# Issue orders of ACT, DVE and the queue in a fused attention and convolution step: five places moved

## The chip, the cores and the metric

The kernel runs on one core of a Trainium2 chip. The metric is the device time of one execution in microseconds (us); three runs were taken, and their median counts. The engines are PE (TensorE), DVE (VectorE), ACT (ScalarE), POOL (GpSimd) and SP (SyncE, which issues the transfers). In the rows of the profile PEld is the weight load of PE and SPq the issue on SP's queue.

## The reference, cut to what matters

```python
h = x / rms(x) * norm_g                              # x: 1024 prompt frames, 32 sample frames; D = 1024
q, k, v, f, ga, ua, ub, gb, ma, mb = split(h @ w_in) # each 1024 wide, f 16
q, k = rmsnorm(q) * q_g / 8, rmsnorm(k) * k_g        # per head, 16 heads of 64
o = softmax(q k^T + C[t] - C[s], causal) v           # C = cumsum(logsigmoid(f + b_f))
conv = depthwise(ua * sigmoid(ub), 31 taps, causal)  # conv state in front for the sample frames
ya = (o * silu(ga)) @ w_pa
yb = (silu(layernorm(conv)) * silu(gb)) @ w_pb
y = x + (sigmoid(ma) * ya + sigmoid(mb) * yb) @ w_out
# outputs: y, k, v, logsigmoid(f), last 30 conv rows; the sample frames attend over 512 cached ones too
```

All of it is f32.

## The kernel before

Every f32 product is made of three fp32r matmuls. A value is split into a high part (a cast to fp32r on ACT) and a low part (value minus high part, on POOL for weights, on DVE or POOL for activations), and PE adds high x high, low x high and high x low (`mms`, L102, in the profile `pj<-xh,wh`, `pj<-xh,wl`, `pj<-xl,wh`). A block is 128 output channels: 8 contraction slices (kt) times 3 column thirds of 352 frames times 3 matmuls, 72 in all, with its own weights of 128 x 1024: one load of `raw` (L85), one cast to `wh` (L91), three subtractions to `wl` (L94).

In the order of time the stages are:

- `x_split` (L413 to L510): transposes of x (`ptx`, L436), its split into `xh` and `xl` (L438, L439) and the first convolution input. The roots of the rows' mean squares come from `newton` (L375 to L379), called for rows 256 to 639 as `steps_of[2]` behind slice 5; the `scale` calls (L407, L409) multiply rows of x by them, and the transposes of the next chunk read those.
- the blocks of u, v, k and q, with the 30 convolution taps of each channel block on DVE (L265) beside them. Finished taps are summed for the LayerNorm (`into_sums`, L236 to L248): a sum on DVE, a square on ACT (L242), a sum of squares.
- the eight ga blocks, then the opening of the attention: `most(h, j)` (L917 to L932) makes the scores of 128 queries against their keys (`psS`, L924, one PSUM bank for j under 4, two from 4 on), adds the causal mask on the last 128 keys (L927) and takes the negative maximum `nm` (L932); `least` (L934) transposes the maxima and writes them into the query tile `QA` (L937).
- sixteen heads, each in four steps of PE work: weights (`psT`, L946, L947, masked on DVE in L950; exponential on ACT into `pt`, L953; running sums `acc` on POOL, L956, L959), products with V (`po`, L970), the scores of the next head's maxima, and between them matmuls of the gate blocks gb, ma, mb (`fill`). Of the 24 gate blocks (numbered 0 to 23) 22 go between the heads. With every second head `sums` (L978 to L1000) makes the row sums of two heads on PE (`pl`, L982), their logarithm (L984) and reciprocal (L994) on ACT, the product `rs` with silu(ga) on POOL (L997) and the product with the heads' output `ot` on DVE (L998), one half at each of its steps, and the store `s_o` (L1000).
- gate blocks 22 and 23, and meanwhile `a_half` (L1165): the attention output comes back from `s_o` and is split into `ah` (ACT, L1169) and `al` (DVE, L1170), one slice for each 128 channels.
- `outproj` (L1202) for pa, pb and out, 8 blocks each (pa0 to pa7 and so on). Block 0 goes slice by slice over all three thirds, since its input is only just being made; the others third by third. Beside pa, `ln_out` (L1174) makes the LayerNorm output `c_h`, `c_l` from the kept convolution: DVE (L1178, L1179, L1182), SiLU on ACT (L1180, L1181), cast on ACT (L1186), subtraction on POOL (L1187). `mk_pa` loads the gate ma in three thirds and takes tanh on ACT (L1222); DVE multiplies PE's result by it (L1225).

The order on PE is the order of the code. On ACT, DVE, POOL and SP a scheduler sets it for the first stage, the attention and what follows, by priorities (`high_priority` puts the weights' load, cast and subtractions forward) and by `issue_after`, which puts an instruction behind another one of its engine. Raw weights rotate over a list of pools, `rawp`: `load_raw` takes the first and puts it at the end (L83 to L85). The list has the pools of the projections until `rawp.extend` (L1156) adds two, ahead of the last two gate blocks.

Of the kernel before, what the change touches and what calls it, by code (L numbers as in the profile page):

```python
# [48 lines left out]
def build(tc, xT, xt, wv, wf, ckT, cv, clT, stT, vec, cst, yT, kT, vO, lfO, cpT, csT):  # L49
# [38 lines left out]
    def split_w(raw, offset=2000):  # L88
        with tc.high_priority(offset=offset):
            wh = wp.tile([128, KT, 128], F32R, name="wh", tag="wh")  # L90
            nc.scalar.copy(wh, raw)  # L91
            wl = wp.tile([128, KT, 128], F32R, name="wl", tag="wl")
            for k0, k1 in WSP:
                nc.gpsimd.tensor_sub(wl[:, k0:k1, :], raw[:, k0:k1, :], f32(wh[:, k0:k1, :]))  # L94
        return wh, wl
# [11 lines left out]

    late = []
    chores = []
    pace = {"tick": 0, "n": 0, "rate": 0.0, "credit": 0.0}  # L110

    def later(n, fn):
# [88 lines left out]
            taps.pop(0)()  # L201

    PCS = ((0, T, 0), (T + 30, TS, T))
    sides = {}

    def shift_of(y):

# [28 lines left out]
    def into_sums(f, y):  # L236
        for o, n, a in PCS:
            if f == 0:
                nc.vector.tensor_copy(mean[:, a:a + n], y[:, o:o + n])
            else:  # L240
                nc.vector.tensor_add(mean[:, a:a + n], mean[:, a:a + n], y[:, o:o + n])
        nc.scalar.activation(y, y, AF.Square)  # L242
        eng = nc.vector if f == 6 else nc.gpsimd
        for o, n, a in PCS:
            if f == 0:
                eng.tensor_copy(rstd[:, a:a + n], y[:, o:o + n])
            else:
                eng.tensor_add(rstd[:, a:a + n], rstd[:, a:a + n], y[:, o:o + n])  # L248
        if f == 7:
            sides["ready"] = True  # L250
# [105 lines left out]
    def vcol(base, f):  # L356
        return vec_t[:, base + f:base + f + 1]
# [17 lines left out]
    def newton(out, v, y):  # L375

        nc.vector.tensor_mul(out, y, y)
        nc.vector.scalar_tensor_tensor(out, out, -0.5, v, op0=ALU.mult, op1=ALU.mult)
        nc.vector.scalar_tensor_tensor(out, out, 1.5, y, op0=ALU.add, op1=ALU.mult)  # L379

    half = slice(0, D // 2), slice(D // 2, D)
    rows = lambda t: min(128, TT - 128 * t)
# [27 lines left out]

    behind = []

    def x_split(c, ws, u, jobs):  # L413


        o, n = XCH[c]
# [16 lines left out]
        for kt in range(KT):  # L433
            pt = tr.tile([128, 512], F32, name="ptx", tag="tr") if kt % 3 == 2 else st.tile([128, 512], F32, name="ptx", tag="st")
            for j in range((n + 127) // 128):
                nc.tensor.transpose(pt[:, 128 * j:128 * j + 128],  # L436
                                    xtok[o // 128 + j][:, 128 * kt:128 * kt + 128], ident)
            nc.scalar.mul(xh[:, kt, sl], pt[:, :n], vcol(V_NG, kt))  # L438
            nc.vector.scalar_tensor_tensor(xl[:, kt, sl], pt[:, :n], vcol(V_NG, kt), f32(xh[:, kt, sl]),  # L439
                                           op0=ALU.mult, op1=ALU.subtract)  # L440
            for job in jobs.get(kt, ()):
                job()
            behind.append(lambda kt=kt: project(kt))
            if len(behind) > 2:
                behind.pop(0)()
# [41 lines left out]
    for f in range(8):  # L487
# [9 lines left out]
        3: [lambda: squares(3, sl=half[0]), lambda: squares(3, False, half[1], part),  # L497
            lambda: V.tensor_add(rs9[:, 3:4], rs9[:, 3:4], part)],
        4: [lambda: rooted(2, 3)],
        5: [lambda: steps_of[2](), lambda: scale(2, 0), lambda: scale(3, 0, True), lambda: scale(4, 0)],  # L500
        6: [lambda: scale(3, 1, True), lambda: scale(2, 1)],
        7: [lambda: scale(4, 1)]})
    x_split(1, ws0, u0, {
        0: [lambda: squares(5), lambda: squares(6, False)],
        1: [lambda: squares(7)],
# [405 lines left out]
    class Attend:  # L911
# [66 lines left out]
        def sums(self, other):  # L978
# [11 lines left out]
            for i, (c, e, acc) in enumerate(four):  # L990
                for u in range(2):
                    q = 64 * e + 32 * u
                    with tc.issue_after(sides["weights"].ins):
                        nc.scalar.activation(rs[c][q:q + 32, :], ln[32 * i:32 * i + 32, :], AF.Exp, scale=-1.0)  # L994
                if e:
                    osl = slice(c * 512, c * 512 + 512)
                    nc.gpsimd.tensor_mul(rs[c], rs[c], self.g[:, osl])  # L997
                    nc.vector.tensor_mul(ot[:, osl], ot[:, osl], rs[c])  # L998
                yield
            nc.sync.dma_start(s_o[self.head.h // 2, :, :T], ot)  # L1000

    PT = [ap.tile([128, 4 * n, 512], F32, name=f"pt{n}", bufs=1) for n in (1, 2)]
# [50 lines left out]
                att[h].most(j)  # L1053

    for j in range(4):
        most(0, j, 4 + j)
        fill(8 if j == 3 else 4)
    att[0].least(0)
    att[0].least(1)
# [2 lines left out]
    for h in range(H):  # L1062
# [4 lines left out]
        for s in range(4):  # L1067
# [35 lines left out]
            elif s == 2:  # L1103
                most(h + 1, 3)
                most(h + 1, 5)
                fill(2)
                if k - 2 in sample:
                    sample[k - 2].turn()
# [44 lines left out]
    pjC = Banks3()  # L1153
    sg2 = pool("sg2", 4, stack=p3, side="right")
    bg = pool("bg", 5, stack=p3, side="right")
    rawp.extend(pool(f"rw{i}", 1, stack=p3, side="right") for i in range(2))  # L1156

    def big(name):
        return bg.tile([128, TT], F32, name=name, tag="big")
# [34 lines left out]
        a_half(f)  # L1194
    while fills:
        last_gate()

    def ln_step(f):
        for g in LNO[f - 1]:
# [2 lines left out]
    def outproj(g, rh, rl, mk, between=lambda f: None):  # L1202

        w = split_w(load_raw((g, 0)))
        pss = [pjC.tile([128, CH], F32, name="pj", tag="pj") for _ in range(3)]
        for kt in range(KT):
            for c in range(3):
# [2 lines left out]
        with tc.high_priority(offset=4000):  # L1210
            for c in range(3):
                ev(c, csl(c), pss[c])
        for f in range(1, 8):
            between(f)
            proj((g, f), rh, rl, pjC, mk(f))


    def mk_pa(f):
        sma = [sg2.tile([128, CH], F32, name="sma", tag="sma") for _ in range(3)]
        for c in range(3):  # L1220
            nc.sync.dma_start(sma[c], s_g["ma"][f, :, csl(c)])
            nc.scalar.activation(sma[c], sma[c], AF.Tanh, scale=0.5)  # L1222

        def ev(c, sl, ps):
            nc.vector.scalar_tensor_tensor(sma[c], sma[c], 1.0, ps, op0=ALU.add, op1=ALU.mult)  # L1225
# [119 lines left out]
```

## Time and profile before

| what | us |
|---|---|
| three runs | 1391.07, 1395.28, 1392.76 |
| median | 1392.76 |
| the profiled execution | 1393.11 |
| its span, first to last instruction | 1391.0 |
| PE busy | 1367.7 (98%) |
| DVE, POOL, ACT busy | 895.2, 704.6, 567.3 |

The mean granted clock of PE was 0.996. A row of the timeline is start, duration, engine, line, operation, output and inputs, shapes, count, and in brackets the idle time ahead of it with the instruction that ended it. A row of the waits is the waiting engine and line, the one waited for, the total in us, the count, and the longest.

### The profile page before, as it was taken

What the parts mean: (1) busy time and instruction counts of PE and PEld (TensorE: products, weight loads), DVE (VectorE), ACT (ScalarE), POOL (GpSimd) and SP (SyncE); (2) the same over time, 40 slices, a digit from 0 to 9 for tenths busy, and PEclk for the clock granted to TensorE, in tenths of its full rate; (3) what the DMA queues carried; (4) which work ended last, traced back from release to release, by engine and by line L of the source; (5) the groups of instructions that cost most, each with busy time, mean ns of one, the idle gap of its engine ahead of it and who ended that gap; (6) DMA issues with size and microseconds to landing.
All of it is one profiled execution on the core that took longest, in us unless ns stands there. A gap on an engine that the chain in (4) does not pass through costs nothing.

```text
span 1391.0 us, 22743 instructions
## 1 busy us (share of the span) xinstructions
PE 1367.7 (98%) x8707; PEld 1277.9 (92%) x8707; DVE 895.2 (64%) x1173; ACT 567.3 (41%) x1061; POOL 704.6 (51%) x589
## 2 busy tenths in 40 slices
PE   8999999999999999999999999999999999999999
PEld 8999999999999999998777887878887899999998
DVE  6787787888898998757766675854553496133111
ACT  6422334646464642223434445443543665222100
POOL 3334254567585875336645664554554466255320
PEclk9999999999999999999999999999999999999999
DMA  4342343534342475234546655565642877444431
GB/s 184 98 143 88 123 113 103 161 89 138 103 158 90 129 196 161 88 111 105 151 119 173 143 137 137 135 172 138 159 116 77 298 252 259 139 151 141 143 107 48
DMA packets 102797, 193.85 MB, mean 139 GB/s; under 512 B 17504, under 2 KB 70624, under 8 KB 102688
## 3 DMA queue, kind: packets, MB, share of 16 engines
q1 hardware_dynamic: 102544, 192.32, 46.5%
q8 instruction: 69, 1.13, 0.3%
q14 instruction: 40, 0.33, 0.1%
q10 hardware_dynamic: 144, 0.07, 0.0%
HBM read 126.17 MB, written 66.17 MB: 138 GB/s over the span
## 4 chain that ended last, share of the span: by engine, by line
PE 88%; DVE 5%; ACT 2%; issue 2%; DMA 1%; POOL 1%; SPq 0%; DVEq 0%; ACTq 0%; POOLq 0%
PE pj L102 66%; PE pjv L591 7%; PE po L970 5%; PE psS L924 2%; PE psT L947 2%; PE psT L946 2%; DVE nm L932 1%; PE pl L982 1%; PE pst L708 1%; DVE y L265 1%; PE pst L707 1%; PE ptx L436 0%; ACT acc L994 0%; POOL wl L94 0%; PE po L908 0%
## 5 line engine op out<-in xcount | busy, mean ns | idle before, releaser
L102 PE MATMUL pj<-xh,wh 128*128 128x352 f32 (+2 forms) x1536 | 505.8, 329 | 4.5 <-ACT wh L91 3.7
L102 PE MATMUL pj<-xl,wh 128*128 128x352 f32 (+2 forms) x1536 | 496.5, 323 | 0.5 <-DVE xl L439 0.3
L102 PE MATMUL pj<-xh,wl 128*128 128x352 f32 (+2 forms) x1536 | 495.4, 323 | 1.5 <-POOL wl L94 1.5
L94 POOL TENSOR_TENSOR wl<-raw,wh 128x384 fp32r<-128x384 f32 (+1 forms) x258 | 323.8, 1282 | 331.9 <-ACT wh L91 303.0
L265 DVE SCALAR_TENSOR_TENSOR y<-u,vec_t,y 128x1086 f32<-128x1086 f32 x240 | 385.1, 1605 | 23.9 <-ACT y L262 19.6
L102 PEld LDWEIGHTS pj<-xh,wh 128*128 128x128 f32 x1536 | 289.6, 189 | 14.0 <-ACT wh L91 4.3
L102 PEld LDWEIGHTS pj<-xh,wl 128*128 128x128 f32 x1536 | 290.6, 189 | 3.0 <-POOL wl L94 2.2
L102 PEld LDWEIGHTS pj<-xl,wh 128*128 128x128 f32 x1536 | 290.1, 189 | 1.7 <-DVE xl L439 1.6
L959 POOL TENSOR_TENSOR acc<-acc,pt 128x512 f32<-128x512 f32 (+3 forms) x128 | 125.4, 980 | 38.7 <-ACT pt L953 32.7
L91 ACT CAST wh<-raw 128x1024 fp32r<-128x1024 f32 x86 | 90.0, 1046 | 108.9 <-PE pj L102 78.3
L953 ACT ACTIVATE pt<-psT 128x512 f32<-128x512 f32 x192 | 83.5, 492 | 43.1 <-DVE psT L950 18.0
L725 POOL TENSOR_TENSOR ql<-qn,qh 128x352 fp32r<-128x352 f32 (+1 forms) x48 | 65.9, 1372 | 65.9 <-ACT qh L724 53.1
L932 DVE TENSOR_REDUCE nm<-psS 128x1 f32<-128x128 f32 (+7 forms) x128 | 93.5, 751 | 1.8
L956 POOL TENSOR_TENSOR acc<-pt 128x512 f32<-128x512 f32 x32 | 44.7, 1398 | 80.2 <-ACT pt L953 80.2
L763 ACT COPY t<-pj 128x352 f32<-128x352 f32 x72 | 32.6, 452 | 129.1 <-PE pj L102 65.8
L927 DVE TENSOR_TENSOR psS<-psS,cmask 128x128 f32<-128x128 f32 x128 | 37.3, 296 | 61.5 <-PE psS L924 59.1
L970 PE MATMUL po<-pt,V 128*64 128x512 f32 (+1 forms) x384 | 73.2, 530 | 0.0
L591 PE MATMUL pjv<-vwh,xh 128*128 128x260 f32 x256 | 72.5, 283 | 0.0
L591 PE MATMUL pjv<-vwl,xh 128*128 128x260 f32 x256 | 72.4, 283 | 0.0
L591 PE MATMUL pjv<-vwh,xl 128*128 128x260 f32 x256 | 72.3, 282 | 0.0
L970 PEld LDWEIGHTS po<-pt,V 128*64 128x64 f32 x384 | 26.4, 138 | 43.3 <-issue 40.0
L1255 DVE SCALAR_TENSOR_TENSOR xres<-pj,xres 128x352 f32<-128x352 f32 x24 | 12.5, 525 | 80.4 <-PE pj L102 76.9
(215 smaller groups left out, 2399.7 us busy)
## 6 DMA issues: line engine op xcount, KB each, us to landing
raw<-wf SPq DMA_DIRECT2D x88, 512.0 KB
QB<-s_q SPq DMA_DIRECT2D x32, 256.0 KB
KB<-s_k SPq DMA_DIRECT2D x32, 256.0 KB
kT<-qn SPq DMA_DIRECT2D x8, 528.0 KB
s_ga<-t SPq DMA_DIRECT2D x24, 176.0 KB
s_gb<-t SPq DMA_DIRECT2D x24, 176.0 KB
s_ma<-t SPq DMA_DIRECT2D x24, 176.0 KB
s_mb<-t SPq DMA_DIRECT2D x24, 176.0 KB
```

Source lines behind the costliest of these rows:

```text
L91: nc.scalar.copy(wh, raw)
L94: nc.gpsimd.tensor_sub(wl[:, k0:k1, :], raw[:, k0:k1, :], f32(wh[:, k0:k1, :]))
L102: nc.tensor.matmul(ps, a[:, kt, :], b(kt, sl), start=(first and n == 0), stop=(last and n == N - 1))
L265: t = nc.vector.scalar_tensor_tensor(y, u[:, i:i + CW], w, y, op0=ALU.mult, op1=ALU.add)
L591: nc.tensor.matmul(ps[:, :VC], a, b, start=(n == 0), stop=(n == 23))
L725: nc.gpsimd.tensor_sub(ql[:, :n], qn[:, o], f32(qh[:, :n]))
L927: nc.vector.tensor_add(diag, diag, cmask)
L932: nc.vector.tensor_reduce(nm[:, r:r + 1], ps[:, :nb, :w], axis=AX.XY, op=ALU.max, negate=True)
L953: sides['weights'] = nc.scalar.activation(p[:, j, q0:], ps[:, q0:], AF.Exp)
L956: nc.gpsimd.tensor_add(self.acc[c], p[:, 0, :], p[:, 1, :])
L959: nc.gpsimd.tensor_add(a[:, q0:], a[:, q0:], p[:, j, q0:])
L970: nc.tensor.matmul(po[64 * o:64 * o + 64, q0:], V[:, j + o, hd], p[:, j + o, q0:], start=(j == 0), stop=(j == njb - 2), skip_group_check=True)
```

## The change

The edits are:

- `into_sums`: the square on ACT is put behind the cast of weights issued last before it (`sides["wh"]`).
- `x_split`: the three root operations of rows 256 to 639 go ahead of the `xl` of slice 5 instead of behind it.
- the opening: `most(0, 4 + j, j)` in place of `most(0, j, 4 + j)`.
- `sums`: the two products with `ot` come in two further steps behind the four reciprocals, and the attention loop takes one more step in its part s == 2.
- the two added raw pools join the rotation behind the last gate block, at its front.
- `outproj("pa")`: the weights of pa1 are loaded and split right behind pa0's, and those of block f + 1 ahead of the LayerNorm steps in front of block f (`split[g, f]` is where `proj` finds weights already split); and each tanh of ma is put behind the cast issued last.

```diff
--- before.py
+++ after.py
@@ -88,7 +88,7 @@
     def split_w(raw, offset=2000):
         with tc.high_priority(offset=offset):
             wh = wp.tile([128, KT, 128], F32R, name="wh", tag="wh")
-            nc.scalar.copy(wh, raw)
+            sides["wh"] = nc.scalar.copy(wh, raw)
             wl = wp.tile([128, KT, 128], F32R, name="wl", tag="wl")
             for k0, k1 in WSP:
                 nc.gpsimd.tensor_sub(wl[:, k0:k1, :], raw[:, k0:k1, :], f32(wh[:, k0:k1, :]))
@@ -107,6 +107,7 @@
 
     late = []
     chores = []
+    sides = {}
     pace = {"tick": 0, "n": 0, "rate": 0.0, "credit": 0.0}
 
     def later(n, fn):
@@ -201,7 +202,6 @@
             taps.pop(0)()
 
     PCS = ((0, T, 0), (T + 30, TS, T))
-    sides = {}
 
     def shift_of(y):
 
@@ -239,7 +239,8 @@
                 nc.vector.tensor_copy(mean[:, a:a + n], y[:, o:o + n])
             else:
                 nc.vector.tensor_add(mean[:, a:a + n], mean[:, a:a + n], y[:, o:o + n])
-        nc.scalar.activation(y, y, AF.Square)
+        with tc.issue_after(sides["wh"].ins):
+            nc.scalar.activation(y, y, AF.Square)
         eng = nc.vector if f == 6 else nc.gpsimd
         for o, n, a in PCS:
             if f == 0:
@@ -376,7 +377,7 @@
 
         nc.vector.tensor_mul(out, y, y)
         nc.vector.scalar_tensor_tensor(out, out, -0.5, v, op0=ALU.mult, op1=ALU.mult)
-        nc.vector.scalar_tensor_tensor(out, out, 1.5, y, op0=ALU.add, op1=ALU.mult)
+        return nc.vector.scalar_tensor_tensor(out, out, 1.5, y, op0=ALU.add, op1=ALU.mult)
 
     half = slice(0, D // 2), slice(D // 2, D)
     rows = lambda t: min(128, TT - 128 * t)
@@ -410,7 +411,7 @@
 
     behind = []
 
-    def x_split(c, ws, u, jobs):
+    def x_split(c, ws, u, jobs, ahead={}):
 
 
         o, n = XCH[c]
@@ -436,8 +437,11 @@
                 nc.tensor.transpose(pt[:, 128 * j:128 * j + 128],
                                     xtok[o // 128 + j][:, 128 * kt:128 * kt + 128], ident)
             nc.scalar.mul(xh[:, kt, sl], pt[:, :n], vcol(V_NG, kt))
-            nc.vector.scalar_tensor_tensor(xl[:, kt, sl], pt[:, :n], vcol(V_NG, kt), f32(xh[:, kt, sl]),
-                                           op0=ALU.mult, op1=ALU.subtract)
+            with ExitStack() as first:
+                if kt in ahead:
+                    first.enter_context(tc.issue_after(ahead[kt]().ins))
+                nc.vector.scalar_tensor_tensor(xl[:, kt, sl], pt[:, :n], vcol(V_NG, kt), f32(xh[:, kt, sl]),
+                                               op0=ALU.mult, op1=ALU.subtract)
             for job in jobs.get(kt, ()):
                 job()
             behind.append(lambda kt=kt: project(kt))
@@ -497,9 +501,9 @@
         3: [lambda: squares(3, sl=half[0]), lambda: squares(3, False, half[1], part),
             lambda: V.tensor_add(rs9[:, 3:4], rs9[:, 3:4], part)],
         4: [lambda: rooted(2, 3)],
-        5: [lambda: steps_of[2](), lambda: scale(2, 0), lambda: scale(3, 0, True), lambda: scale(4, 0)],
+        5: [lambda: scale(2, 0), lambda: scale(3, 0, True), lambda: scale(4, 0)],
         6: [lambda: scale(3, 1, True), lambda: scale(2, 1)],
-        7: [lambda: scale(4, 1)]})
+        7: [lambda: scale(4, 1)]}, {5: lambda: steps_of[2]()})
     x_split(1, ws0, u0, {
         0: [lambda: squares(5), lambda: squares(6, False)],
         1: [lambda: squares(7)],
@@ -993,10 +997,13 @@
                     with tc.issue_after(sides["weights"].ins):
                         nc.scalar.activation(rs[c][q:q + 32, :], ln[32 * i:32 * i + 32, :], AF.Exp, scale=-1.0)
                 if e:
-                    osl = slice(c * 512, c * 512 + 512)
-                    nc.gpsimd.tensor_mul(rs[c], rs[c], self.g[:, osl])
-                    nc.vector.tensor_mul(ot[:, osl], ot[:, osl], rs[c])
+                    nc.gpsimd.tensor_mul(rs[c], rs[c], self.g[:, c * 512:c * 512 + 512])
                 yield
+            for c in range(2):
+                osl = slice(c * 512, c * 512 + 512)
+                nc.vector.tensor_mul(ot[:, osl], ot[:, osl], rs[c])
+                if c == 0:
+                    yield
             nc.sync.dma_start(s_o[self.head.h // 2, :, :T], ot)
 
     PT = [ap.tile([128, 4 * n, 512], F32, name=f"pt{n}", bufs=1) for n in (1, 2)]
@@ -1053,7 +1060,7 @@
                 att[h].most(j)
 
     for j in range(4):
-        most(0, j, 4 + j)
+        most(0, 4 + j, j)
         fill(8 if j == 3 else 4)
     att[0].least(0)
     att[0].least(1)
@@ -1103,6 +1110,7 @@
             elif s == 2:
                 most(h + 1, 3)
                 most(h + 1, 5)
+                next(norm, None)
                 fill(2)
                 if k - 2 in sample:
                     sample[k - 2].turn()
@@ -1153,7 +1161,7 @@
     pjC = Banks3()
     sg2 = pool("sg2", 4, stack=p3, side="right")
     bg = pool("bg", 5, stack=p3, side="right")
-    rawp.extend(pool(f"rw{i}", 1, stack=p3, side="right") for i in range(2))
+    more = [pool(f"rw{i}", 1, stack=p3, side="right") for i in range(2)]
 
     def big(name):
         return bg.tile([128, TT], F32, name=name, tag="big")
@@ -1194,6 +1202,7 @@
         a_half(f)
     while fills:
         last_gate()
+    rawp[:0] = more
 
     def ln_step(f):
         for g in LNO[f - 1]:
@@ -1202,6 +1211,8 @@
     def outproj(g, rh, rl, mk, between=lambda f: None):
 
         w = split_w(load_raw((g, 0)))
+        if g == "pa":
+            split[g, 1] = split_w(load_raw((g, 1)))
         pss = [pjC.tile([128, CH], F32, name="pj", tag="pj") for _ in range(3)]
         for kt in range(KT):
             for c in range(3):
@@ -1211,6 +1222,8 @@
             for c in range(3):
                 ev(c, csl(c), pss[c])
         for f in range(1, 8):
+            if g == "pa" and f < 7:
+                split[g, f + 1] = split_w(load_raw((g, f + 1)))
             between(f)
             proj((g, f), rh, rl, pjC, mk(f))
 
@@ -1219,7 +1232,8 @@
         sma = [sg2.tile([128, CH], F32, name="sma", tag="sma") for _ in range(3)]
         for c in range(3):
             nc.sync.dma_start(sma[c], s_g["ma"][f, :, csl(c)])
-            nc.scalar.activation(sma[c], sma[c], AF.Tanh, scale=0.5)
+            with tc.issue_after(sides["wh"].ins):
+                nc.scalar.activation(sma[c], sma[c], AF.Tanh, scale=0.5)
 
         def ev(c, sl, ps):
             nc.vector.scalar_tensor_tensor(sma[c], sma[c], 1.0, ps, op0=ALU.add, op1=ALU.mult)

```

The orders below are those of the built kernels, before and then after. First ACT from the last head's weights (L763 copies a gate block's result; L953 and L957 are the same line, as are L975 and L979, L984 and L988, L994 and L998, and L763 and L767) to gate block 23. Before:

```order
L763 COPY t<-pj 128x352
L953 ACTIVATE pt_6454<-psT 128x512
L953 ACTIVATE pt_6454<-psT 128x384
L953 ACTIVATE pt_6454<-psT 128x256
L953 ACTIVATE pt_6454<-psT 128x128
L975 COPY ot<-po 64x512 x2
L984 ACTIVATE acc<-pl 128x512
L994 ACTIVATE acc<-acc 32x512 x4
L994 ACTIVATE rs<-acc 32x512 x4
L763 COPY t<-pj 128x352 x3
L91 CAST wh<-raw 128x1024 x2
```

After:

```order
L767 COPY t<-pj 128x352
L91 CAST wh<-raw 128x1024
L957 ACTIVATE pt_6454<-psT 128x512
L957 ACTIVATE pt_6454<-psT 128x384
L957 ACTIVATE pt_6454<-psT 128x256
L957 ACTIVATE pt_6454<-psT 128x128
L979 COPY ot<-po 64x512 x2
L988 ACTIVATE acc<-pl 128x512
L998 ACTIVATE acc<-acc 32x512 x4
L998 ACTIVATE rs<-acc 32x512 x4
L767 COPY t<-pj 128x352 x3
L91 CAST wh<-raw 128x1024
```

The cast of gate block 23 stood behind the last reciprocals and shared a row with pa0's; now it stands ahead of the last four exponentials, and pa0's is alone. POOL at the same place, before:

```order
L959 TENSOR_TENSOR acc<-acc,pt_6454 128x512 x3
L959 TENSOR_TENSOR acc<-acc,pt_6454 128x384
L959 TENSOR_TENSOR acc<-acc,pt_6454 128x256
L959 TENSOR_TENSOR acc<-acc,pt_6454 128x128
L997 TENSOR_TENSOR acc<-acc,ga 128x512
L997 TENSOR_TENSOR rs<-rs,ga 128x512
L94 TENSOR_TENSOR wl<-raw,wh 128x384 x2
L94 TENSOR_TENSOR wl<-raw,wh 128x256
```

After (L963 is L959, L1000 is L997):

```order
L963 TENSOR_TENSOR acc<-acc,pt_6454 128x512 x2
L94 TENSOR_TENSOR wl<-raw,wh 128x384 x2
L94 TENSOR_TENSOR wl<-raw,wh 128x256
L963 TENSOR_TENSOR acc<-acc,pt_6454 128x512
L963 TENSOR_TENSOR acc<-acc,pt_6454 128x384
L963 TENSOR_TENSOR acc<-acc,pt_6454 128x256
L963 TENSOR_TENSOR acc<-acc,pt_6454 128x128
L1000 TENSOR_TENSOR acc<-acc,ga 128x512
L1000 TENSOR_TENSOR rs<-rs,ga 128x512
L94 TENSOR_TENSOR wl<-raw,wh 128x384 x2
L94 TENSOR_TENSOR wl<-raw,wh 128x256
```

The three subtractions of gate block 23 moved ahead of the last four additions of the running sum.

DVE in the middle of head 4 (L998 and L1004 are the product of `ot`, L265 and L266 the tap, L932 and L936 the maximum, L950 and L954 the mask of `psT`). Before:

```order
L927 TENSOR_TENSOR psS<-psS,cmask 128x128 x2
L932 TENSOR_REDUCE nm_7865<-psS 128x1
L932 TENSOR_REDUCE nm_7887<-psS 128x1
L265 SCALAR_TENSOR_TENSOR y<-u,vec_t,y 128x1086
L950 TENSOR_TENSOR psT<-psT,kmask 128x128 x2
L998 TENSOR_TENSOR ot<-ot,rs 128x512
L927 TENSOR_TENSOR psS<-psS,cmask 128x128
L937 TENSOR_TENSOR QA<-pm,ident 4x512
L932 TENSOR_REDUCE nm_7887<-psS 128x1
```

After:

```order
L931 TENSOR_TENSOR psS<-psS,cmask 128x128 x2
L936 TENSOR_REDUCE nm_7864<-psS 128x1
L936 TENSOR_REDUCE nm_7886<-psS 128x1
L954 TENSOR_TENSOR psT<-psT,kmask 128x128 x2
L1004 TENSOR_TENSOR ot<-ot,rs 128x512
L266 SCALAR_TENSOR_TENSOR y<-u,vec_t,y 128x1086
L931 TENSOR_TENSOR psS<-psS,cmask 128x128
L941 TENSOR_TENSOR QA<-pm,ident 4x512
L936 TENSOR_REDUCE nm_7886<-psS 128x1
```

The tap that stood ahead of the mask of `psT` and the product stands behind the product now, ahead of the score's mask and the maximum.

ACT around pa5's cast of weights (the one cast of weights in each list; L1180 and L1188 are the SiLU of the LayerNorm output, L1181 and L1189 that of gb, L1222 and L1236 the tanh, L1186 and L1194 the cast of `c_h`). Before:

```order
L1186 CAST c_h<-y_11998 128x1056
L1181 ACTIVATE g_12108<-g_12108 128x1056
L1222 ACTIVATE sma<-sma 128x352
L1180 ACTIVATE y_12107<-y_12107,vec_t 128x1056
L91 CAST wh<-raw 128x1024
L1186 CAST c_h<-y_12107 128x1056
L1181 ACTIVATE g_12217<-g_12217 128x1056
L1222 ACTIVATE sma<-sma 128x352 x2
```

After:

```order
L1188 ACTIVATE y_12014<-y_12014,vec_t 128x1056
L1189 ACTIVATE g_12124<-g_12124 128x1056
L1194 CAST c_h<-y_12014 128x1056
L91 CAST wh<-raw 128x1024
L1188 ACTIVATE y_12123<-y_12123,vec_t 128x1056
L1236 ACTIVATE sma<-sma 128x352 x2
L1194 CAST c_h<-y_12123 128x1056
L1189 ACTIVATE g_12233<-g_12233 128x1056
```

Before, the cast stood right behind a SiLU of the LayerNorm output; now one such SiLU and two tanh come behind it.

## The prediction

> **What bounds the kernel now.** I read the page first: which engine is full, and how much of the span it is not.
>
> ```profile
> span 1391.0 us, 22743 instructions
> PE 1367.7 (98%) x8707; PEld 1277.9 (92%) x8707; DVE 895.2 (64%) x1173; ACT 567.3 (41%) x1061; POOL 704.6 (51%) x589
> ```
>
> TensorE (PE) is idle for 1391.0 - 1367.7 = 23.3 us. Its instructions are the same 8707 afterwards, so an edit that gains must shorten those 23.3 us or make the matmuls themselves quicker. The waits of PE say whom it waits for (total us, times, longest):
>
> ```profile
> PE psS L924 <- DVE nm L932: 6.9, 8, 2.1
> PE pj L102 <- ACT wh L91: 3.7, 2, 2.8
> PE pj L102 <- POOL wl L94: 3.2, 5, 0.8
> PE ptx L436 <- DVE xl L439: 1.5, 1, 1.5
> ```
>
> These four are 15.3 us of the 23.3. All edits aim at one of them. There is a second price, which busy time hides; stretches of the trace (length, then busy us and instructions of PE, PEld, DVE, ACT, POOL, then the granted clock, DMA share, GB/s) show it:
>
> ```profile
> 21.80:25.10 3.30, 3.30 (x24) 3.23 (x24) 2.38 (x5) 3.30 (x9) 0.00 (x0) 1.00 0.00 0
> 588.50:591.80 3.30, 3.30 (x13) 3.30 (x12) 0.00 (x0) 0.38 (x1) 3.30 (x8) 0.50 0.94 304
> 697.80:701.10 3.30, 3.30 (x12) 1.68 (x12) 0.52 (x1) 0.00 (x0) 1.69 (x3) 0.50 1.01 223
> 1093.70:1097.00 3.30, 3.30 (x14) 3.30 (x12) 3.27 (x7) 2.28 (x3) 3.30 (x5) 0.50 1.04 410
> 1105.80:1117.30 11.50, 11.50 (x72) 11.50 (x72) 7.94 (x7) 8.06 (x8) 4.77 (x3) 1.00 0.96 353
> ```
>
> Three times the granted clock is 0.50 for a stretch of 3.3 us and PE starts 12 to 14 matmuls where the 72 of the last row, 11.50 us, would make it 20.7. Each stands right behind waits:
>
> ```profile
> 19.74 0.44 PE L436 MATMUL ptx<-ident,xtok 128*128 128x128 f32 x2 [1.48 <-DVE xl L439]
> 588.18 0.43 PE L102 MATMUL pj<-xh,wl 128*128 128x352 f32 x1 [0.82 <-POOL wl L94]
> 696.02 0.71 PE L924 MATMUL psS<-KA,QA 72*128 72x512 f32 x2 [2.11 <-DVE nm L932]
> ```
>
> The 1.48 is followed by 1.00 (the row from 21.80). The 0.82, with the other wait for ACT's cast just before it (3.7 - 2.8 = 0.9), makes 1.7 and is followed by 0.50, as are the 2.11 here and gate 23's below. So waits that add up to 1.7 us or more bring a second loss, half of a stretch of 3.4 us, 1.7; 1.5 us does not.
>
> **The last gate's weights: where most of it lies.** Gate 23 stands between the last head and outproj("pa"). Queue, casts and PE there:
>
> ```profile
> 1050.92 0.33 SPq L85 DMA_DIRECT2D raw<-wf  x1
> 1086.20 1.24 SPq L85 DMA_DIRECT2D raw<-wf  x2
> 1090.65 1.04 ACT L91 CAST wh<-raw 128x1024 fp32r<-128x1024 f32 x1 [1.23 <-DMA raw<-wf]
> 1091.74 0.43 PE L102 MATMUL pj<-xh,wh 128*128 128x352 f32 x1 [2.82 <-ACT wh L91]
> 1092.82 0.43 PE L102 MATMUL pj<-xh,wl 128*128 128x352 f32 x1 [0.65 <-POOL wl L94]
> ```
>
> The slot loaded at 1050.92 goes to block pa1, and gate 23 shares the loads at 1086.20 with pa0. With the two new buffers joined to the rotation only after the gates, gate 23 takes the load at 1050.92. PE was free for it at 1091.74 - 2.82 = 1088.92 and began pa0 at 1105.80: 16.9 us for what takes 11.5 in the row of pa0 above. Of the 5.4, 2.82 + 0.65 = 3.5 are waits and 1.9 the 0.50 clock at 1093.70. I take all of it as removed (bounds 3.5, if a 0.50 stretch appears anyway, to 5.4): **+5.2**, a tenth of the clock part held back.
>
> The cast and its three subtractions move into the last head. What covers them:
>
> ```profile
> 1068.82 0.45 ACT L763 COPY t<-pj 128x352 f32<-128x352 f32 x1 [0.39 <-ACT pts L897]
> 1069.70 0.98 ACT L953 ACTIVATE pt<-psT 128x512 f32<-128x512 f32 x2 [0.43 <-DVE psT L950]
> 1070.44 3.71 POOL L959 TENSOR_TENSOR acc<-acc,pt 128x512 f32<-128x512 f32 x4 [3.11 <-ACT pt L953]
> 1076.19 1.07 PE L982 MATMUL pl<-acc,ones_f 128*32 128x512 f32 x8
> 1176.18 2.67 POOL L94 TENSOR_TENSOR wl<-raw,wh 128x384 fp32r<-128x384 f32 x3
> 1164.23 4.78 POOL L94 TENSOR_TENSOR wl<-raw,wh 128x384 fp32r<-128x384 f32 x3 [3.84 <-issue]
> ```
>
> ACT: 1069.27 + 1.04 = 1070.3, so the exponentials behind it slip from 1069.70 by 0.6 and are needed by PE only in the output products ahead of pl. POOL: the subtractions (2.67 when undisturbed) from 1070.4 to 1073.1, then the four additions, 3.71, to 1076.8. The last row sums (pl) on PE start within 1076.19 to 1077.26, and the last of them needs the last addition: 0 to 0.5 late, counted 0. SP: the load stands where pa1's stood, so nothing else there is later.
>
> What is late next is the attention output's low half, al. PE would reach pa0 5.4 earlier, at 1100.4, and walks it by contraction slices (kt), 11.5/8 = 1.44 us each; slice 5 is due at 1100.4 + 5 x 1.44 + 0.3 (its third product) = 1107.9.
>
> ```profile
> 1102.27 1.28 ACT L1222 ACT_TABLE_LOAD   x1
> 1107.33 2.05 ACT L1169 CAST ah<-a 128x1056 fp32r<-128x1056 f32 x2
> 1108.43 4.96 DVE L1170 TENSOR_TENSOR al<-a,ah 128x1056 fp32r<-128x1056 f32 x3 [4.88 <-ACT ah L1169]
> ```
>
> Slices 5 to 7 of al are made from 1108.43, 1.65 each. ACT now has pa1's cast (1.04), the table load (1.28) and three tanh ahead of cast 5, and the first of these waits for gate 23's last output, 5.4 earlier: cast 5 ends between 1103 (if it all shifts with PE) and 1108.4 (if the loads of a hold it where it was). al 5 then ends 1104.6 to 1110.1 against 1107.9: a wait of 0 to 3. Middle of the later half, because the loads of a follow the queue and not PE: **-1.2**.
>
> **outproj("pa"): split earlier, tanh behind casts.**
>
> ```profile
> 1165.37 0.43 PE L102 MATMUL pj<-ah,wl 128*128 128x352 f32 x1 [0.78 <-POOL wl L94]
> 1190.51 0.43 PE L102 MATMUL pj<-ah,wl 128*128 128x352 f32 x1 [0.70 <-POOL wl L94]
> 1161.89 1.27 ACT L1180 ACTIVATE y<-y,vec_t 128x1056 f32<-128x1056 f32 x1 [2.67 <-DVE y L1179]
> 1187.89 0.50 ACT L1222 ACTIVATE sma<-sma 128x352 f32<-128x352 f32 x1 [1.42 <-DMA sma<-s_ma]
> 1188.30 1.03 ACT L91 CAST wh<-raw 128x1024 fp32r<-128x1024 f32 x1
> ```
>
> The casts of pa5 and pa7 (1188.30) stood right behind a SiLU that itself waited 2.67 for DVE and a tanh that waited 1.42 for its load. Now pa5's cast stands ahead of the next SiLU, and pa7's ahead of two of the tanh. The L94 waits are 3.2 in all; less the 0.65 of gate 23 and the 0.82 at 588.18, which stays, they are 1.7 here, and they go. But PE comes 4 us earlier, while VectorE and GpSimd, which make the LayerNorm output between these blocks, do not get faster: the subtractions of pa5, 4.78 against 2.67, show them in each other's way. A later chain could hold PE again, for 0 to 4; nearest is the 0.78 of now, half of it: 0.4. Sum **+1.3**. The tanh that now come later feed only VectorE's products, whose PSUM banks are seven deep.
>
> **Output products two steps later.** PE, ACT, POOL and SP keep their order; on DVE three heads change. The rows are head 4's, with one of head 2 (687) and of head 6 (813):
>
> ```profile
> 752.06 2.33 POOL L997 TENSOR_TENSOR rs<-rs,ga 128x512 f32<-128x512 f32 x1
> 754.43 1.75 DVE L998 TENSOR_TENSOR ot<-ot,rs 128x512 f32<-128x512 f32 x1 [0.78 <-POOL rs L997]
> 687.31 1.30 POOL L997 TENSOR_TENSOR rs<-rs,ga 128x512 f32<-128x512 f32 x1
> 758.37 0.47 PE L924 MATMUL psS<-KA,QA 72*128 72x512 f32 x1 [0.73 <-DVE nm L932]
> 813.80 0.47 PE L924 MATMUL psS<-KA,QA 72*128 72x512 f32 x1 [0.55 <-DVE nm L932]
> ```
>
> Head 4: the convolution tap (1.46 here) moves from ahead of the product to behind it, ahead of the maximum that PE waits for. If the product keeps its start, 754.43, the wait becomes 0.73 + 1.46 = 2.2, with a 0.50 stretch 3.9; if POOL's 2.33 that gates the product, 1.30 without a tap beside it, shrinks by 1.0, the product starts at 753.4 and takes less, and the wait is near 0. Head 2: the product goes ahead of a tap and waits for POOL, 0.4 more on the 2.11 that stays. Head 6: a tap and QA's scaling leave the way, -0.5. Together between -3 and +0.5; I take **-0.3**, near the second case, since the tap that stretched POOL's row is what leaves.
>
> **The small ones.**
>
> ```profile
> 16.99 0.48 DVE L439 SCALAR_TENSOR_TENSOR xl<-ptx,vec_t,xh 128x256 fp32r<-128x256 f32 x1 [0.87 <-ACT xh L438]
> 607.86 0.44 PE L924 MATMUL psS<-KA,QA 72*128 72x448 f32 x1 [0.45 <-DVE nm L932]
> ```
>
> Roots first: three operations 3 elements wide go ahead of this xl of 0.48, in its idle 0.87, in front of the 1.48 wait: bounds 0 and 0.5, **+0.25**. Opening: PE makes the two-bank score first; the 0.45 may go, but not the first wait for ACT: 0 to 0.45, **+0.2**. The square behind a cast: the latest cast issued already stands ahead of every square on ACT, whose order there is unchanged: **0**, and the 588.50 stretch with its waits stays.
>
> **Sum.** 5.2 - 1.2 + 1.3 - 0.3 + 0.25 + 0.2 = 5.45. The profiled execution took 1393.11 (span 1391.0 and 2.1 around it): 1387.7. It lies 0.35 over the median, 1392.76; from that, 1387.3. I say 1387.4.
>
> **Rivals.**
> - *Eaten downstream* (the gain is PE's early arrival at pa0, given back): al 3 late plus LayerNorm's chain holding pa5 and pa6 for up to 2 more leaves 5.45 - 1.8 - 2 = 1.6: 1391. For it: VectorE's al row at 1108.43 and POOL's 4.78. Against: pa's waits are all under 0.8 now. It decides once cast 5 ends after 1107.5.
> - *No clock to be won.* If the 0.50 stretches belong to something else than the preceding wait, only 3.5 of the 5.4 goes: 5.45 - 1.7 = 3.75, 1389.0. Against it stand three stretches that each begin within 2 us of a wait. By the Trainium skill, "TensorE: Matmul & The Clock Gate", section "What's actually happening", the half clock comes after at least one whole idle window of about 3.4 us; by that rule waits of 2 to 3 us would cost no clock, and the time would be this rival's. The trace disagrees, with 0.50 in the 697.80 row after 2.11.
> - *Slower: POOL before the row sums.* The subtractions of gate 23 stand ahead of the last head's additions. At 4.78 in place of 2.67, and with additions stretched like POOL's 2.33 against 1.30, 3.71 becomes 6.6: pl waits 2.1 + 2.9 + 0.6 = 5.6, plus a 0.50 stretch 1.7, is 7.3 against a gain of 5.45: 1394.6. It turns the sign from 3.8 of wait with the stretch. Against: VectorE has almost nothing to do there. The same place gives more if the raw load lands after 1069.3.
> - *Attention turns worse*: head 4 at -3.9 and head 2 with a larger wait: 1391.
>
> **Chances.** A difference under 0.3% (4.2 us: under 1388.6 is faster, over 1396.9 slower) can't be told from no change. Forecast (1384 to 1389) 0.60; eaten downstream 0.20; no clock 0.06; attention 0.08; POOL before the row sums 0.06, half of it beyond 1396.9 with a late load. Faster: most of the first, 0.56; slower 0.03; same 0.41. The range for 8 in 10 is 1384.0 to 1392.0: up to the eaten gain and a little past it, down to 5.4 + 1.7 + 0.5 + 0.45 + 0.5 = 8.6 with nothing given back.
>
> **What would show it.** Right: gate 23 follows gate 22 without a wait and no 0.50 stretch near 1093; PE starts pa0 about 1100; a wait of one to two us on al from DVE in pa0; the L94 waits of pa gone or under 0.5; at 588 the same waits and stretch; the 1.5 of L436 at about 1.2; head 4's wait under 0.7. Wrong: waits on pl, waits of pa over 1.7 with 0.50 behind them, or 0.50 behind head 4.

## The result, and the profile after

The changed kernel takes 1387.82 us (median of 7, 1386.21 to 1389.38) against 1392.67 (7 runs) in the same comparison: ratio 0.9967, 95% interval 0.9956 to 0.9979, so 2.9 to 6.1 us less. Forecast were 1387.4 and 5.45 less. The profiled execution has a span of 1385.6, 5.4 under that of before. The page, and the waits of PE (total us, times, longest):

```profile
span 1385.6 us, 22743 instructions
PE 1365.7 (99%) x8707; PEld 1275.7 (92%) x8707; DVE 888.5 (64%) x1173; ACT 567.1 (41%) x1061; POOL 701.8 (51%) x589
```

```profile
PE psS L928 <- DVE nm L936: 7.5, 7, 2.3
PE pj L102 <- POOL wl L94: 1.6, 4, 0.8
...
PE ptx L437 <- DVE xl L443: 1.2, 1, 1.2
PE psT L950 <- DVE ot L980: 1.1, 1, 1.1
PE pj L102 <- ACT wh L91: 0.9, 1, 0.9
```

PE's idle time is 19.9 us, 3.4 less; its busy time is 2.0 less with the same matmuls, which goes with the granted clock: 0.999 in place of 0.996, one half-clock stretch in place of three. The waits for ACT's casts (3.7 before) and for POOL's subtractions (3.2) gave 4.4; the waits for DVE's maxima grew from 6.9 to 7.5, and one for DVE's `ot` is new.

The start of each matmul set against the same matmul of before shows where the difference steps: -0.3 at the first chunk's xl; +1.0 at 540 to 543, of which 0.3 is a wait on POOL and the rest was not traced; -1.5 at 588 to 592; -0.2 in the opening; +1.8 over the attention; +0.4 at the row sums pl; -5.6 over gate block 23; -1.1 in outproj("pa"). Between these the two run in step to within 0.2. Their sum is -5.5.

Gate block 23, in rows of the timeline of SP, ACT, POOL and PE, and behind them the block itself as a stretch (length, then busy us and instructions of PE, PEld, DVE, ACT, POOL, granted clock, DMA share, GB/s):

```profile
1051.80 0.33 SPq L85 DMA_DIRECT2D raw<-wf  x1
1070.06 1.05 ACT L91 CAST wh<-raw 128x1024 fp32r<-128x1024 f32 x1
1071.18 2.64 POOL L94 TENSOR_TENSOR wl<-raw,wh 128x384 fp32r<-128x384 f32 x3 [2.96 <-ACT wh L91]
1073.77 3.69 POOL L963 TENSOR_TENSOR acc<-acc,pt 128x512 f32<-128x512 f32 x4
1077.08 1.48 PE L986 MATMUL pl<-acc,ones_f 128*32 128x512 f32 x8
```

```profile
1090.05:1101.50 11.45, 11.45 (x74) 11.45 (x73) 5.78 (x11) 6.29 (x8) 2.86 (x3) 1.00 1.02 377
```

The load is early, the cast stands ahead of the exponentials, and the block takes 11.45 at full clock in place of 16.9. POOL's additions end at 1077.46, and pl lasts 1.48 against 1.07: that is the 0.4 that comes back.

The half-clock stretches at the places where before had them, and at head 4:

```profile
589.20:592.50 3.30, 3.30 (x21) 3.30 (x22) 0.00 (x0) 0.55 (x1) 3.30 (x8) 1.00 0.92 302
696.90:700.20 3.30, 3.30 (x11) 1.96 (x11) 0.72 (x1) 0.00 (x0) 1.89 (x4) 0.50 1.04 232
759.00:762.30 3.30, 3.30 (x18) 2.50 (x20) 2.79 (x4) 0.55 (x2) 1.20 (x2) 1.00 0.97 257
```

At 589 the same waits as before (0.88 and 0.83) are followed by full clock this time, which is the -1.5; at 759 a wait of 2.02 is not followed by half clock. That is taken up with the pauses below.

The attention's loss, on POOL, DVE, ACT and PE, at head 4 and where head 7 begins:

```profile
751.33 1.29 POOL L1000 TENSOR_TENSOR rs<-rs,ga 128x512 f32<-128x512 f32 x1
752.58 4.98 POOL L963 TENSOR_TENSOR acc<-acc,pt 128x512 f32<-128x512 f32 x3
752.65 1.76 DVE L1004 TENSOR_TENSOR ot<-ot,rs 128x512 f32<-128x512 f32 x1 [0.16 <-POOL rs L1000]
754.34 2.37 DVE L266 SCALAR_TENSOR_TENSOR y<-u,vec_t,y 128x1086 f32<-128x1086 f32 x1
758.90 0.47 PE L928 MATMUL psS<-KA,QA 72*128 72x512 f32 x1 [2.02 <-DVE nm L936]
819.62 1.33 DVE L234 TENSOR_TENSOR y<-y,shift 128x1024 f32<-128x1024 f32 x2 [3.69 <-DMA s_y<-y]
821.46 1.21 DVE L241 TENSOR_TENSOR mean<-mean,y 128x1024 f32<-128x1024 f32 x1
822.81 1.11 ACT L243 ACTIVATE y<-y 128x1086 f32<-128x1086 f32 x1 [4.50 <-DVE mean L241]
823.83 0.56 ACT L979 COPY ot<-po 64x512 f32<-64x512 f32 x1
824.42 0.68 DVE L980 TENSOR_TENSOR ot<-ot,po 64x512 f32<-64x512 f32 x1 [0.93 <-ACT ot L979]
825.16 0.33 PE L950 MATMUL psT<-QB,KB 128*128 128x128 f32 x1 [1.11 <-DVE ot L980]
```

At head 4 POOL's `rs` shrinks from 2.33 to 1.29 and the product starts earlier, as one of the two cases of the forecast had it. But the product takes 1.76 where it took 1.75 before, and the tap behind it 2.37 in place of 1.46, while POOL adds its running sums all along (the row of 752.58). Where no POOL operation runs beside them, the product takes 0.67 to 0.69 in this trace (5 of 16) and the tap 1.33 to 1.35 (83 of 240). The wait grows from 0.73 to 2.02. At head 6 the wait of 0.55 is gone. Behind it a wait of 1.11 is new: the last tap ends later, so does its store and the sums for the LayerNorm, and the square (L243, 822.81) still stands on ACT ahead of the copy (L979, 823.83) for which DVE's L980 waits, and PE waits for L980.

### The profile page after: what moved, and what is told of

It is laid out like the page before. It is cut to its first block, busy times and chain, and to the rows that moved or that the text cites. A ratio compares the mean times of both kernels' runs of the same rounds, so it can differ in the third digit from the quotient of the medians.

```text
span 1385.6 us, 22743 instructions
## 1 busy us (share of the span) xinstructions
PE 1365.7 (99%) x8707; PEld 1275.7 (92%) x8707; DVE 888.5 (64%) x1173; ACT 567.1 (41%) x1061; POOL 701.8 (51%) x589
## 4 chain that ended last, share of the span: by engine, by line
PE 85%; DVE 5%; POOL 3%; DMA 2%; ACT 2%; issue 1%; SPq 0%; ACTq 0%; DVEq 0%; POOLq 0%
PE pj L102 63%; PE pjv L595 7%; PE po L974 5%; PE psS L928 2%; PE psT L951 2%; PE psT L950 2%; POOL wl L94 2%; POOL c_l L1195 1%; DVE y L266 1%; DVE nm L936 1%; DMA a<-s_o 1%; PE warm L355 1%; PE pl L986 1%; DMA g<-s_gb 1%; PE pst L712 1%
## 5 line engine op out<-in xcount | busy, mean ns | idle before, releaser
L94 POOL TENSOR_TENSOR wl<-raw,wh 128x384 fp32r<-128x384 f32 (+1 forms) x258 | 320.4, 1269 | 330.0 <-ACT wh L91 310.3
L266 DVE SCALAR_TENSOR_TENSOR y<-u,vec_t,y 128x1086 f32<-128x1086 f32 x240 | 385.9, 1608 | 23.7 <-ACT y L263 19.3
L963 POOL TENSOR_TENSOR acc<-acc,pt 128x512 f32<-128x512 f32 (+3 forms) x128 | 127.2, 994 | 37.5 <-ACT pt L957 31.5
L957 ACT ACTIVATE pt<-psT 128x512 f32<-128x512 f32 x192 | 83.4, 492 | 42.6 <-DVE psT L954 17.5
L936 DVE TENSOR_REDUCE nm<-psS 128x1 f32<-128x640 f32 (+7 forms) x128 | 93.4, 751 | 1.8
L767 ACT COPY t<-pj 128x352 f32<-128x352 f32 x72 | 32.6, 452 | 128.8 <-PE pj L102 70.4
L950 PE MATMUL psT<-QB,KB 128*128 128x512 f32 x192 | 64.5, 343 | 1.1 <-DVE ot L980 1.1
```

The lines of the kernel that those rows point to most:

```text
L266: t = nc.vector.scalar_tensor_tensor(y, u[:, i:i + CW], w, y, op0=ALU.mult, op1=ALU.add)
L936: nc.vector.tensor_reduce(nm[:, r:r + 1], ps[:, :nb, :w], axis=AX.XY, op=ALU.max, negate=True)
L950: nc.tensor.matmul(ps[:, q0:], KB[:, ks], QB[:, qs], start=True, stop=False)
L957: sides['weights'] = nc.scalar.activation(p[:, j, q0:], ps[:, q0:], AF.Exp)
L963: nc.gpsimd.tensor_add(a[:, q0:], a[:, q0:], p[:, j, q0:])
```

## The experiments

### One edit alone: the buffer, outproj("pa"), the output products

**The buffer.**

```diff
-    rawp.extend(pool(f"rw{i}", 1, ...) for i in range(2))
+    more = [pool(f"rw{i}", 1, ...) for i in range(2)]
...
     while fills:
         last_gate()
+    rawp[:0] = more
```

> The kernel before with one edit alone: the two raw buffers join the rotation behind the last gate block. Theory A (the gain is gate 23's own): 5.5 us go at gate 23 (3.5 of waits, 0.3 of refilling, 1.7 of half clock), 0.4 come back at the row sums pl: 5.1 less than before, ratio 0.9963. Rival B (eaten downstream without the earlier casts): PE comes 5 us earlier to an unchanged pa, al and the LayerNorm chain hold it there, the waits on L94 in pa grow from 1.7 to over 3.5 and the gain is 3 or less, ratio 0.9978 or more.

Measured: 1385.55 (5 runs), ratio 0.9956 (0.9943 to 0.9969), 6.1 us less (4.3 to 7.9). Theory A: its 5.1 lies in the interval. The profiled execution (span 1381.0) is 10.0 shorter, but two more half-clock stretches of before, those at 588 and 697, are not in it either. The main rest of PE's waits in this kernel:

```profile
PE psS L924 <- DVE nm L932: 6.5, 8, 2.1
PE ptx L436 <- DVE xl L439: 1.5, 1, 1.5
...
PE pj L102 <- POOL wl L94: 1.1, 2, 0.8
PE pj L102 <- ACT wh L91: 0.8, 1, 0.8
```

Of the L94 waits, 3.2 before, the 0.8 at 588 and one of 0.3 are left: the waits of 0.78 and 0.70 in pa are gone, without the edit that was made for them. In the order of ACT the casts of pa stand earlier once gate block 23 no longer takes one of the new buffers. pa5's row here,

```profile
1149.57 1.05 ACT L91 CAST wh<-raw 128x1024 fp32r<-128x1024 f32 x1
```

is 6.6 us ahead of PE's first matmul of pa5 (1156.17); before, it was 1.2 ahead (1163.07 and 1164.23).

**outproj("pa").**

```diff
+        if g == "pa":
+            split[g, 1] = split_w(load_raw((g, 1)))
...
+            if g == "pa" and f < 7:
+                split[g, f + 1] = split_w(load_raw((g, f + 1)))
             between(f)
...
+            with tc.issue_after(sides["wh"].ins):
                 nc.scalar.activation(sma[c], sma[c], AF.Tanh, scale=0.5)
```

> The kernel before with the edit of outproj("pa") alone (weights split earlier, tanh behind casts). Theory A: the three waits of pa (0.78, 0.26, 0.70) go: 1.7 less, ratio 0.9988. Rival B: PE was held there by VectorE's and GpSimd's LayerNorm chain and not by the casts' place, other waits of the same size come: 0 to 0.5 less, ratio above 0.9995.

Measured: 1391.36 (11 runs), ratio 0.9993 (0.9983 to 1.0004): no difference that can be told, which is the size of B. PE's waits and the timeline of ACT and PE at pa5:

```profile
PE pj L102 <- ACT wh L91: 3.4, 2, 2.6
PE pj L102 <- POOL wl L94: 2.9, 5, 0.8
```

```profile
1158.45 1.27 ACT L1180 ACTIVATE y<-y,vec_t 128x1056 f32<-128x1056 f32 x1 [2.67 <-DVE y L1179]
1159.62 1.03 ACT L91 CAST wh<-raw 128x1024 fp32r<-128x1024 f32 x1
1161.92 0.43 PE L102 MATMUL pj<-ah,wl 128*128 128x352 f32 x1 [0.79 <-POOL wl L94]
```

pa5's cast still stands right behind the SiLU that waits 2.67 for DVE, and PE still waits 0.79. The wait of 0.70 at pa7 is gone, one of 0.38 at pb0 has come. So B's cause is not shown by this kernel: the place of pa5's cast did not change in it, and where the cast does stand earlier, with the buffer alone, the wait is gone, as theory A had it.

**The output products.**

```diff
-                    nc.vector.tensor_mul(ot[:, osl], ot[:, osl], rs[c])
                 yield
+            for c in range(2):
+                osl = slice(c * 512, c * 512 + 512)
+                nc.vector.tensor_mul(ot[:, osl], ot[:, osl], rs[c])
+                if c == 0:
+                    yield
...
+                next(norm, None)
```

> The kernel before with the output products two steps later alone. Theory A (the trace after): 1.3 more at head 4's maximum, 0.7 less at head 6's, 1.4 more at the weights that open head 7, 0.3 less later: 1.8 more than before, ratio 1.0013. Rival B (the prediction's term): 0.3 more, ratio 1.0002, the 1.4 being the neighbour edits' and not in this kernel.

Measured: 1395.74 (11 runs), ratio 1.0025 (1.0015 to 1.0036), 3.5 us slower. Theory A in direction and place. Its own profile has the steps +1.24 at head 4, -0.71 at head 6, +1.50 at head 7, -0.33 later and +0.17 at head 2, 1.9 in all, with these waits:

```profile
PE psS L924 <- DVE nm L932: 7.4, 7, 2.3
...
PE psT L946 <- DVE ot L976: 1.1, 1, 1.1
```

So the new wait at head 7 belongs to this edit. The rest of the 3.5 is not in this profile. It is the fastest of the eleven runs (1391.91, granted clock 0.999): the half-clock stretches that before has behind 696 and in gate block 23 are not in it, and its span, 1389.8, is even 1.2 under that of before. The clocks of the runs point to the rest: their median is 0.995, against 0.997 in the 21 runs of before beside them, which is 2.8 us by an estimate (0.002 of 1391, good to 1.4 since the clock is listed to 0.001). One place for it is known: behind the wait of 2.0 at head 4 the two kernels with pauses (below), which carry this edit too, show a half-clock stretch, worth 1.7, and this profile does not.

### The change without two of its edits

The first kernel is the changed one with the diff of the output products taken back, the second has that of outproj("pa") taken back too:

```diff
-            for c in range(2):                   # first and second
-                ... ot[:, osl] * rs[c]
-                next(norm, None)                 # in s == 2
-        if g == "pa":                            # second alone
-            split[g, 1] = split_w(load_raw((g, 1)))
-            with tc.issue_after(sides["wh"].ins):  # around tanh
```

> The changed kernel with the output products where they were before. Theory A: the 1.8 that the trace after shows in the attention go, and stay gone: 1386.0. Rival B: PE comes to pa0 1.8 earlier, the attention output's low half (al), which in the changed kernel was ready within 0.2 of when PE needed it, then holds PE because its loads follow the queue: 1387.5 or more, with a wait on DVE's al of over 1 us in pa0.

Measured: 1385.46 (5 runs), ratio 0.9958 (0.9945 to 0.9970) to the kernel before. The interval overlaps that of the change (0.9956 to 0.9979), so the profile decides, for theory A: it shows the attention's steps reversed (-1.24, +0.67, -1.40) and no wait on al of over 0.2. PE comes to pa0 earlier and al with it.

> The changed kernel with the output products and outproj("pa") as they were before: left are the last gate's buffer, the roots, the opening and the square. Theory A (with gate 23 early, pa's casts are no longer late, as the kernel with the buffer alone showed: its waits of 0.78 and 0.70 were gone without the pa edit): the same as with the pa edit, 1385.5, waits on L94 in pa under 0.5 in all. Rival B (the pa edit is worth its 1.3 of the prediction): 1386.8, with waits of 0.7 to 0.8 on L94 in pa.

Measured: 1384.55 (5 runs), ratio 0.9950 (0.9935 to 0.9964). Theory A: with the buffer in place the pa edit is worth nothing that can be measured. The interval overlaps that of the kernel with it, and its waits say the same:

```profile
PE pj L102 <- POOL wl L94: 1.1, 2, 0.8
...
PE pj L102 <- DVE al L1174: 0.2, 1, 0.2
```

The roots, the opening and the square were not run alone. This kernel has the three beside the buffer, and its ratio, 0.9950, can't be told from that of the buffer alone, 0.9956.

### The square behind the cast of ga7's weights

```diff
-        with tc.issue_after(sides["wh"].ins):
+        def square():
             nc.scalar.activation(y, y, AF.Square)
             ...                                   # and its sums
+        if f == 6:
+            later(6, square)
+        else:
+            square()
```

> The changed kernel with the output products as before, and the square of the seventh channel block (f = 6) issued six matmul groups later in the code, so that on ACT it stands behind the cast of block ga7's weights. Theory A: the two waits before ga7 (0.7 and 0.8) go, and with them the half-clock stretch that follows them in some executions (1.7): 1.5 to 3.2 less than the same kernel without it (1385.5), so 1382.3 to 1384.0. Rival B: the cast then waits for its own load or for PE's old block, and 0 to 0.5 is won.

Measured: 1382.04 (5 runs), ratio 0.9932 (0.9919 to 0.9946) to the kernel before, by the medians 3.4 us below the same kernel without it (1385.46, measured apart; its interval, 0.9945 to 0.9970, begins where this one ends). Theory A, 0.3 under its range. ACT's rows before, where the square stands ahead of the cast of ga7's weights, and in this kernel, where that cast is the first and the square comes after it:

```profile
584.83 1.11 ACT L242 ACTIVATE y<-y 128x1086 f32<-128x1086 f32 x1 [9.68 <-DVE mean L241]
585.85 1.03 ACT L91 CAST wh<-raw 128x1024 fp32r<-128x1024 f32 x1
```

```profile
576.53 1.05 ACT L91 CAST wh<-raw 128x1024 fp32r<-128x1024 f32 x1
585.47 0.47 ACT L770 ACTIVATE t<-pj 128x352 f32<-128x352 f32 x1 [7.88 <-DMA s_ga<-t]
587.60 1.11 ACT L243 ACTIVATE y<-y 128x1086 f32<-128x1086 f32 x1 [1.67 <-DVE mean L241]
```

The cast is at 576.5, over 9 us before it was (585.85), and PE has no wait at all on a cast of weights left, and 0.7 on L94, none over 0.3. Its median is the lowest of the study, though its interval overlaps those of the kernel without both edits and of the buffer alone.

### What a wait costs in clock: 14 long pauses against 28 short ones

```diff
+    def pause():
+        ...                                       # two transposes of gf into ps
+            for _ in range(6):                    # 3 in the short one
+                nc.vector.tensor_copy(gf, ps[:, :256])
+        nc.tensor.transpose(pt[:, :128], gf[:, :128], ident)
```

> The changed kernel with 14 pauses of PE, one ahead of each of blocks 1 to 7 of pb and out: two transposes, six copies on DVE of their result, one transpose that reads the last copy. Each pause is a wait of about 2.6 us. Theory A (idle time of half a window of 3.4 us or more brings a window at half clock): 9 to 13 of the 14 pauses are followed by a 0.50 stretch of 3.413 us, and the time is 14 x 2.6 + 11 x 1.7 = 55 over the changed kernel. Rival B (the Trainium skill, TensorE: Matmul & The Clock Gate, section What's actually happening: half clock only after a whole idle window): no stretch at 0.50 behind the pauses, 37 over.

> The same with 28 pauses of three copies each, half of them ahead of the blocks and half in the middle, 5.7 us apart: waits of about 1.4 us. Theory A: none or few are followed by a 0.50 stretch, 28 x 1.4 = 39 over the changed kernel, well under the kernel with 14 long pauses. Rival B: the same as the long ones or a little more, by the added transposes.

Measured: 1462.26 with the long pauses, 1458.39 with the short ones (two runs each). The pauses were longer than meant: the profiles have 14 of 3.3 us on average (the row's 45.9) and 28 of 1.7 (48.6). So the times lie 74 and 71 over the changed kernel, where theory A had 55 and 39, and the stretches decide and not the times. The waits of the long and of the short one, a long pause on PE's timeline, and the stretches in it and behind it:

```profile
PE pj L1218 <- DVE gs L1217: 45.9, 14, 4.7
```

```profile
PE pj L1218 <- DVE gs L1217: 48.6, 28, 3.3
```

```profile
1233.08 0.33 PE L1218 MATMUL pj<-ident,gs 128*128 128x128 f32 x1 [3.33 <-DVE gs L1217]
```

```profile
1230.60:1234.00 3.40, 0.92 (x6) 0.92 (x7) 2.29 (x6) 0.50 (x2) 3.25 (x4) 1.00 0.47 159
1234.10:1237.50 3.40, 3.40 (x13) 3.40 (x12) 0.00 (x0) 0.00 (x0) 0.19 (x1) 0.50 0.88 281
```

Behind the long pauses 14 windows of 3.413 us are at 0.50 (12 of the 14 pauses are followed, two of them by two windows), behind the short ones 4. The short ones have 42 transposes and 2.7 us of waits more, and take 3.9 us less. The stretch before the 0.50 still has 0.92 us of busy PE, so it was no whole idle window. Rival B falls.

By the Trainium skill, "TensorE: Matmul & The Clock Gate", section "What's actually happening", half clock needs a whole idle window of about 3.4 us; the 14 windows at 0.50 disagree, and the measurement decides. That the windows run free of the program, which the same section states, agrees with what follows.

In ten profiles of this study (before, after and eight experiments) I laid the grid of 3.413 us through the stretches at 0.50 (with the buffer alone, which has none, through the first step to full clock) and summed PE's idle time in each window. Of the windows that ran at full clock, all 21 with 1.92 us of idle or more are followed by one at 0.50; none under 1.3 is; from 1.3 to 1.9 both occur (10 with). Two windows that were at 0.50 themselves, with 1.87 and 1.20 us of idle, are followed by another. None of the windows was idle whole: the most was 3.16. That explains the chance in it: the two long pauses without a stretch behind them were cut by the grid into 1.4 and 1.9 and into 1.2 and 1.9; the 2.02 wait at 758.90 was cut by the grid into 1.4 and 0.6, and the two waits before ga7, 1.7 in all, fell into one window before (1.70 of it idle) and into two after.

## Why the prediction was right, by its steps

- **The last gate, +5.2.** Held: 5.6 less 0.4 at pl, 5.2 in the profile. The 0 to 0.5 at pl was named and counted 0.
- **al, -1.2.** Failed: 0.2 was lost. The bounds as written (al 5 ready at 1104.6 to 1110.1, needed at 1107.9) make a wait of 0 to 2.2, not 0 to 3. Cast 5 ended at 1107.9, in the later half that was chosen, but not for the reason given, "because the loads of a follow the queue and not PE": on ACT it stands behind the copy of gate 23's last result, pa1's cast, the table load and three tanh, and so it came with PE, 5.1 to 5.6 us behind PE's first matmul of pa0 in six of the seven profiles with this edit of the buffer (6.6 in that with the long pauses, where PE waits 0.7 for al):

```profile
1102.96 0.44 ACT L767 COPY t<-pj 128x352 f32<-128x352 f32 x1
1106.84 1.07 ACT L1177 CAST ah<-a 128x1056 fp32r<-128x1056 f32 x1
1107.94 2.49 DVE L1178 TENSOR_TENSOR al<-a,ah 128x1056 fp32r<-128x1056 f32 x2 [3.57 <-ACT ah L1177]
```

  PE began pa0 at 1101.50 and not at 1100.4, by the attention's loss, needed slice 5 at 1109.0, and it was there at 1109.2. In the kernel without both edits PE came 2.8 us earlier still, and the wait on al was 0.2.
- **outproj("pa"), +1.3.** The size held (1.1), the cause did not: the buffer alone takes these waits away, the pa edit alone takes one of three. I read the order of the whole change and gave each move to the edit that named it; the order of each edit by itself would have told them apart.
- **Output products, -0.3.** Mis-sized: -1.8 in the profile, 3.5 slower by the runs of the edit alone. The branch was right (POOL's `rs` shrinks, the product starts earlier), but I let the product and the tap run at their undisturbed durations while POOL's additions go on beside them. And the later tap's further road, to the store, the sums, the square on ACT and a PSUM bank, was not followed.
- **Roots +0.25, opening +0.2.** The sizes are as said: 1.48 became 1.2, and the opening gave 0.2. But the opening's wait for the maximum, 0.45, which was to go, is still there with 0.50; where the 0.2 comes from was not traced.
- **The square, 0.** Its order did not move, and the waits stayed at 0.88 and 0.83. The half-clock stretch behind them stayed away in this profile, by the grid and not by the edit.
- **Clock.** The bound of 1.7 was close, but it holds for the idle time in one window, not for a wait. And 1.5 was no safe side: in three of the kernels with the roots' edit (the two without the output products' edit, and that with the square moved) a stretch at 0.50 follows the wait of 1.2 at the first chunk, behind windows with 1.33 to 1.35 us of idle.

That the total came out within 0.6 is luck: al's -1.2, of which 0.2 was paid, and the attention's 1.5 too little nearly cancel, and so do most of two steps that no term covers, -1.5 at 588 and +1.0 at 540. Of the signs named, the wait on al of one to two us did not come, and the wait at head 4, which was to be under 0.7, is 2.02. Of the rivals, "attention turns worse" came true in part: 1.8 in the profile, 3.5 (2.1 to 5.0) by the runs of that edit alone. "Eaten downstream" fell with the buffer alone and the kernels without the products, although its sign came, cast 5 ending after 1107.5.

## What to carry to other kernels

A transfer slot that the last short stage shares with the stage behind it can hold PE longer than any other place: here it held 5.6 us. Who takes which buffer of a rotation is worth writing down for the last blocks before a change of pools. Edits that go through one scheduler have to be ordered and timed one by one, since the one that moves an instruction need not be the one that names it. And an operation that is moved "behind" another must be checked in the order that comes out: here the square did not move until it was issued later in the code, and that was worth about 3.4 us, by medians measured apart. The whole change, with its 0.9967, is no faster than its one edit of the buffer, 0.9956.

## What was not expected of the hardware

The matmul clock's loss goes by idle time in fixed windows of 3.413 us, from somewhere between 1.3 and 1.9 us of it, and not by the length of a single wait: the same waits cost up to 1.7 us more or nothing, by where the grid falls. With 0 to 3 such windows in the profiles of kernels without pauses, this is as large as the spread of the runs of one kernel, 4.2 us for the first three of the kernel before. The clocks listed with the runs fit that roughly: of 21 runs of the kernel before, the three fastest (up to 1390.22) have 0.999 and the slowest (1395.79) 0.995, but one run with 0.948 took 1393.43, which does not fit.
